# Low part of q in 128-row score tiles, adaLN rows in the weight stream's buffers

## The chip, the cores and the metric

The kernel runs on one core of a Trainium2 chip. Time is device microseconds (us) of one execution. In three runs the kernel before took 1821.42, 1823.60 and 1826.22 us; their median is 1823.6 us. A profile of one execution, with every instruction's start and length, stands beside them.

## The reference

One layer of a hybrid backbone on 512 latent tokens (64 x 8 grid, width 1024) and 256 context tokens: an adaLN-modulated norm, one input projection that feeds three mixers (neighbourhood attention, Hyena long convolution, RG-LRU), a gated merge with an output projection, then PEER expert retrieval and a last norm. The part that the change touches is the attention's scores and the modulation vectors:

```python
mod = (jax.nn.silu(c) @ w_ada[l] + b_ada[l]).reshape(B, 1, N_MOD, D)      # six vectors of 1024
s_loc = jnp.einsum('bwhd,bawkhd->bhwak', q_r, k_win) * scale + bias       # 8 heads of 64
s_ctx = jnp.einsum('bwhd,bchd->bhwc', q_r, kc) * scale
s = jnp.concatenate([s_loc, s_ctx], axis=-1)                              # softmax over both
```

All of it is float32, and a product of two operands is made from high and low parts.

## The kernel before

A float32 operand x is split into a high part rounded to the matmul's type (fp32r) and a low part x - high. A product takes three matmuls: high by high, high by low, low by high. `mm3` (lines 221 to 226) does that for the eight 128-row pieces of a weight block, 24 matmuls of 512 columns each. `load_split` (213) brings such a block: `load_raw` (206) loads 128 x 1024 floats by a DMA on SyncE's queue into one of the three buffers `wraw`; ScalarE rounds it into `wh` (line 217), VectorE subtracts into `wl` (218). `wh` and `wl` have two buffers each. A raw buffer is free when line 218 has read it.

The stages around the change, in the order of the program:

- `kproj` (676), interleaved with `rglru` (590): keys of latents and context. A PSUM tile of four 128-column projections is copied by ScalarE (682) and VectorE (683) into `k2` and `kc2`. For each head these hold 128 rows: 64 rows with the high part of k, 64 rows with its low part. For even heads the high part lies in rows 0 to 63, for odd heads in rows 64 to 127.
- The projection of q (730 to 741). `q2` has the high part of q, scaled, in both halves of the rows (738, 739), so that one matmul of 128 rows gives high q by high k plus high q by low k. `ql` has the low part of q (740), the even head of a pair in rows 0 to 63, the odd one in rows 64 to 127 of the same tile.
- `att_gen` (747): for each of four blocks of 128 queries and each of eight heads, `scores` makes a 128 x 512 tile: 256 local keys and 256 context keys. Each half takes one matmul with `q2` (763) and one with `ql` (764), which uses the 64 rows with the high part of k only:

```python
for o, kk in ((0, k2[:, h, kst[qb]:kst[qb] + 256]), (256, kc2[:, h])):
    PE.matmul(p[:, o:o + 256], q2[:, h, qs], kk, start=True, stop=False)
    PE.matmul(p[:, o:o + 256], ql[rows, h // 2, qs], kk[rows], start=False, stop=True)
```

  VectorE adds the bias (765, the bias `bt` comes by a DMA on SyncE's queue, 759) and takes the negative maximum (767), ScalarE the exponential (769), TensorE transposes it (777), ScalarE copies that (779), and TensorE multiplies with v (783). At the end of a block the output is normalised (788) and transposed (793).
- In the same stage, `gate_tanh` (800) for 16 gate blocks (weights `wgate`, 24 matmuls into `pj` each) and 8 blocks `wbrbc` (12 matmuls into `hx` each).
- In the same stage, `mod_gen` (279) for four modulation vectors: eight rows of `w_ada` (128 x 1024 floats, 512 KB each) come by DMAs on SyncE's queue into two buffers `ada` of their own (282, 283), VectorE scales and adds them into `acc` (286, 288), and 8 one-column matmuls sum over the partitions (292). That is 32 loads.

The order of instructions on each engine is not the order of the code: a scheduler takes the whole program, estimates when each instruction could start, and writes each engine's queue and the choice of buffer from that. An engine then runs its queue strictly in order. A row of an engine's queue below is one instruction, or several equal ones.

Of the kernel before, what the change touches and what calls it, by code (L numbers as in the profile page):

```python
# [9 lines left out]
F32 = mybir.dt.float32  # L10
F32R = mybir.dt.float32r
# [9 lines left out]
T = 512  # L21
D = 1024
CT = 256
KD = 8
# [131 lines left out]
def emit(ctx, tc, A, out, dbg=None):  # L156
    nc = tc.nc
    V, S, PE, GP = nc.vector, nc.scalar, nc.tensor, nc.gpsimd
# [47 lines left out]
    def load_raw(src, k=KD, pool=wp):  # L206
        r = pool.tile([128, KD, 128], F32, name="wraw", bufs=3)
        lastld[0] = nc.sync.dma_start(r[:, :k], src)
        return r
# [66 lines left out]
    def bada(m):  # L276
        return vec("bada")[:, m * 8:m * 8 + 8]

    def mod_gen(m, pool, bufs):
        acc = pool.tile([128, D], F32, name="acc", bufs=1)  # L280
        for k in range(KD):
            r = pool.tile([128, D], F32, name="ada", bufs=bufs)
            nc.sync.dma_start(r, A["wada"][m - 2, k])
            w = silu[:, k, 0:1]
            if k == 0:
                V.tensor_scalar(acc, r, w, None, ALU.mult)
            else:
                V.scalar_tensor_tensor(out=acc, in0=r, scalar=w, in1=acc, op0=ALU.mult, op1=ALU.add)
            yield
        ps = hx.tile([128, 512], F32, name="hx")  # L290
        for j in range(8):
            PE.matmul(ps[:, j:j + 1], acc[:, j * 128:j * 128 + 128], onec, start=True, stop=True)
        V.tensor_tensor(mod[:, m, :, 0], ps[:, :8], bada(m), ALU.add)
# [436 lines left out]
    mgs = ctx.enter_context(ExitStack())  # L730
    mg = open_pool(mgs, "mg", side="right")
    q2 = mg.tile([128, 8, T], F32R, name="q2")
    ql = mg.tile([128, 4, T], F32R, name="ql")
    for c in range(4):
        ps, _ = proj(c)
        for i in range(2):
            a_, b_ = slice(64 * i, 64 * i + 64), slice(64 - 64 * i, 128 - 64 * i)
            S.activation(q2[a_, 2 * c + i], ps[a_], AF.Copy, scale=0.125)
            S.activation(q2[b_, 2 * c + i], ps[a_], AF.Copy, scale=0.125)
            V.scalar_tensor_tensor(out=ql[a_, c], in0=ps[a_], scalar=0.125, in1=q2[a_, 2 * c + i],  # L740
                                   op0=ALU.mult, op1=ALU.subtract)

    yah = mg.tile([128, 4, T], F32R, name="yah")
# [3 lines left out]
    def att_gen(ap_):  # L747
        kst = [0, 64, 192, 256]
        vw = [(vt[:, 0], vt[:, 1]), (vs[:, 0], vs[:, 1]), (vs[:, 1], vs[:, 2]), (vt[:, 2], vt[:, 3])]
        for qb in range(4):  # L750
# [1 line left out]
            po = at.tile([128, 512], F32, name="po", bufs=1)  # L752
            bts = []
            def scores(h):
                rows = slice((h % 2) * 64, (h % 2) * 64 + 64)
                p = at.tile([128, 512], F32, name="at")
                if h % BH == 0:
                    bt = ap_.tile([128, BH, 256], F32, name="bt", bufs=2)
                    nc.sync.dma_start(bt, A["nab"][qb, :, h:h + BH])
                    bts.append(bt)  # L760
                qs = slice(qb * 128, qb * 128 + 128)
                for o, kk in ((0, k2[:, h, kst[qb]:kst[qb] + 256]), (256, kc2[:, h])):
                    PE.matmul(p[:, o:o + 256], q2[:, h, qs], kk, start=True, stop=False)
                    PE.matmul(p[:, o:o + 256], ql[rows, h // 2, qs], kk[rows], start=False, stop=True)  # L764
                V.tensor_add(p[:, :256], p[:, :256], bts[-1][:, h % BH])
                nm = ap_.tile([128, 1], F32, name="nm", bufs=3)
                V.tensor_reduce(nm, p, AX.X, ALU.max, negate=True)
                e = ap_.tile([128, 512], F32, name="ae", bufs=2)
                S.activation(e, p, AF.Exp, bias=nm, accum_out=sm[:, h:h + 1])
                return e  # L770
# [35 lines left out]
    with ExitStack() as st:  # L806
# [2 lines left out]

        def late_mods():  # L810
            for m in (2, 4, 3, 5):
                yield from mod_gen(m, ap_, 2)

        lm = late_mods()
        for dc in range(8):
# [490 lines left out]
```

## Time and profile before

| | |
|---|---|
| profiled execution, device time | 1826.02 us |
| its span in the profile | 1824.2 us |
| TensorE busy | 1777.0 us, 97% |
| VectorE busy | 1399.5 us, 77% |
| ScalarE busy | 788.3 us, 43% |
| mean granted TensorE clock | 0.991 of full speed |

The profile names TensorE PE (PEld are its weight loads), VectorE DVE, ScalarE ACT, GpSimd POOL and SyncE's queue SPq. Matmuls overlap in the pipeline and their printed lengths overlap too: the time that a matmul takes from the engine is the distance from its start to the next start. A granted clock of 1.00 is 2.4 GHz, 0.50 is 1.2 GHz. The names in the rows leave buffer numbers out, so `k2` is `k`, `kc2` is `kc`, `q2` is `q`. A float32 matmul that is not fp32r (783, 292) shows as two rows in the trace for one in the program.

### The profile page before, as it was taken

The page shows a single profiled execution, that of the slowest core. Times are in us where ns is not written, and L with a number is a line of the kernel's source. Part 1 is how long each engine was busy: PE and PEld are TensorE (multiplying, and loading weights), DVE is VectorE, ACT ScalarE, POOL GpSimd, SP SyncE. Part 2 cuts the span into 40 slices and gives each one's busy share as a digit, 9 for nine tenths or more (in the row PEclk, how much of TensorE's full clock was granted, in tenths as well). Part 3 has the DMA queues.
Part 4 walks back from the last instruction along what each step waited for, and adds up shares of the span by engine and source line. Part 5 has one row for each costly group of instructions (what it writes and reads, how often), then busy time and mean ns, then how long its engine had stood idle before and what let it go on. Part 6 is the DMA issues. An engine that isn't in the chain of part 4 may idle for free.

```text
span 1824.2 us, 25674 instructions
## 1 busy us (share of the span) xinstructions
PE 1777.0 (97%) x9585; PEld 1543.5 (85%) x9585; DVE 1399.5 (77%) x2550; ACT 788.3 (43%) x1140; POOL 350.9 (19%) x266
## 2 busy tenths in 40 slices
PE   7999999999999999999999999999999999999996
PEld 4688788888878889999999988888888888888885
DVE  6485564555346999999999677888887888788887
ACT  5355553333334324566677533333333333333334
POOL 0000000000000000201011123434443444344451
PEclk9999999999999999999999999999999999999999
DMA  8231522554254224757788899999999999999984
GB/s 311 68 103 47 173 75 89 171 159 130 69 159 139 93 82 138 249 185 280 273 297 290 314 373 326 325 349 334 355 341 346 325 357 340 343 340 333 325 294 155
DMA packets 157677, 431.33 MB, mean 236 GB/s; under 512 B 12784, under 2 KB 62192, under 8 KB 155504
## 3 DMA queue, kind: packets, MB, share of 16 engines
q1 hardware_dynamic: 116224, 257.44, 41.6%
q0 software_dynamic: 36864, 134.23, 20.4%
q10 hardware_dynamic: 4464, 38.01, 5.4%
q8 instruction: 75, 1.23, 0.3%
q14 instruction: 50, 0.41, 0.1%
HBM read 388.48 MB, written 41.16 MB: 236 GB/s over the span
## 4 chain that ended last, share of the span: by engine, by line
PE 87%; DVE 5%; DMA 3%; ACT 2%; issue 2%; POOL 0%; SPq 0%; DVEq 0%; ACTq 0%; POOLq 0%
PE pS L226 9%; PE pS L225 9%; PE pS L224 9%; PE ac L1221 9%; PE ac L1222 9%; PE ac L1220 9%; PE pj L224 6%; PE pj L226 6%; PE pj L225 6%; PE hx L421 2%; PE po L783 2%; DMA gr<-v_rows,idx 1%; PE hx L224 1%; PE hx L225 1%; PE at L764 1%
## 5 line engine op out<-in xcount | busy, mean ns | idle before, releaser
L217 ACT CAST wh<-wraw 128x1024 fp32r<-128x1024 f32 x340 | 350.4, 1032 | 442.2 <-PE pS L225 220.1
L218 DVE TENSOR_TENSOR wl<-wraw,wh 128x1024 fp32r<-128x1024 f32 x340 | 407.3, 1199 | 152.3 <-ACT wh L217 144.4
L1121 POOL DMA_INDIRECT gr<-u_rows,idx x128 | 172.6, 1349 | 1213.2 <-DVE db L1027 744.8
L226 PE MATMUL pS<-zh,wl 128*128 128x384 f32 x1024 | 344.9, 338 | 1.4 <-DVE wl L218 1.4
L224 PE MATMUL pS<-zh,wh 128*128 128x384 f32 x1024 | 344.2, 336 | 1.8 <-ACT sg L1104 1.8
L225 PE MATMUL pS<-zl,wh 128*128 128x384 f32 x1024 | 344.3, 336 | 0.0
L1221 PE MATMUL ac<-wl,ah 128*128 128x512 f32 x768 | 299.4, 390 | 3.1 <-DVE wl L218 3.1
L1222 PE MATMUL ac<-wh,al 128*128 128x512 f32 x768 | 299.0, 390 | 0.0
L1220 PE MATMUL ac<-wh,ah 128*128 128x512 f32 x768 | 276.1, 390 | 1.7 <-ACT wh L217 1.7
L1131 POOL DMA_INDIRECT gr<-v_rows,idx x128 | 171.7, 1341 | 218.0 <-DVE yacc L1137 192.8
L224 PEld LDWEIGHTS pS<-zh,wh 128*128 128x128 f32 x1024 | 192.4, 188 | 5.0 <-ACT sg L1104 2.3
L226 PEld LDWEIGHTS pS<-zh,wl 128*128 128x128 f32 x1024 | 192.2, 188 | 3.4 <-DVE wl L218 2.2
L225 PEld LDWEIGHTS pS<-zl,wh 128*128 128x128 f32 x1024 | 192.4, 188 | 2.7
L1221 PEld LDWEIGHTS ac<-wl,ah 128*128 128x128 f32 x768 | 144.2, 188 | 32.4 <-DVE wl L218 4.4
L1137 DVE SCALAR_TENSOR_TENSOR yacc<-gr,cf,yacc 128x1024 f32<-128x1024 f32 x126 | 160.1, 1280 | 12.6 <-DMA gr<-v_rows,idx 12.6
L1222 PEld LDWEIGHTS ac<-wh,al 128*128 128x128 f32 x768 | 144.2, 188 | 29.6
L1220 PEld LDWEIGHTS ac<-wh,ah 128*128 128x128 f32 x768 | 143.8, 188 | 29.1 <-ACT wh L217 2.0
L1123 DVE SCALAR_TENSOR_TENSOR gr<-gr,xtk 128x1024 f32<-128x1024 f32 x128 | 154.5, 1219 | 0.4 <-DMA gr<-u_rows,idx 0.3
L224 PE MATMUL pj<-xh,wh 128*128 128x512 f32 x336 | 135.2, 402 | 6.3 <-DVE k L683 3.3
L226 PE MATMUL pj<-xh,wl 128*128 128x512 f32 x336 | 135.2, 403 | 0.0
L225 PE MATMUL pj<-xl,wh 128*128 128x512 f32 x336 | 134.7, 401 | 0.0
L1096 ACT COPY stg<-pG 128x512 f32<-128x512 f32 x96 | 99.6, 1164 | 27.7 <-PE pG L1094 27.7
(388 smaller groups left out, 2626.9 us busy)
## 6 DMA issues: line engine op xcount, KB each, us to landing
wraw<-u_cols SPq DMA_DIRECT2D x128, 512.0 KB
wraw<-v_rows SPq DMA_DIRECT2D x128, 512.0 KB
ada<-wada SPq DMA_DIRECT2D x48, 512.0 KB
Gd<-stg ACTq DMA_DIRECT2D x12, 2048.0 KB
gt<-Gd SPq DMA_DIRECT2D x32, 768.0 KB
wraw<-wgate SPq DMA_DIRECT2D x24, 512.0 KB
Sd<-sg ACTq DMA_DIRECT2D x15, 768.0 KB
sgl<-Sd SPq DMA_DIRECT2D x15, 768.0 KB
```

What stands on the lines that cost most here:

```text
L217: S.copy(h[:, :k], r[:, :k])
L218: lsub[0] = V.tensor_sub(l[:, :k], r[:, :k], h[:, :k])
L224: PE.matmul(ps, wh[:, kw], xh[:, kx], start=start and j == 0, stop=False)
L225: PE.matmul(ps, wh[:, kw], xl[:, kx], start=False, stop=False)
L226: PE.matmul(ps, wl[:, kw], xh[:, kx], start=False, stop=stop and j == n - 1)
L1121: GP.indirect_dma_start(out=r, out_offset=None, in_=A["u_rows"], in_offset=bass.IndirectOffsetOnAxis(ap=idx3[:, j:j + 1], axis=0))
L1123: V.scalar_tensor_tensor(out=r, in0=r, scalar=1.0, in1=xtk, op0=ALU.mult, op1=ALU.mult, accum_out=sel3[:, j:j + 1])
L1131: GP.indirect_dma_start(out=r, out_offset=None, in_=A["v_rows"], in_offset=bass.IndirectOffsetOnAxis(ap=idx3[:, j:j + 1], axis=0))
L1137: V.scalar_tensor_tensor(out=a, in0=r, scalar=cf3[:, j:j + 1], in1=a, op0=ALU.mult, op1=ALU.add)
L1220: PE.matmul(ac[t][h], ah[:, ts], vhf[:, hs_], start=j == 0, stop=False)
L1221: PE.matmul(ac[t][h], ah[:, ts], vlf[:, hs_], start=False, stop=False)
L1222: PE.matmul(ac[t][h], al[:, ts], vhf[:, hs_], start=False, stop=j == NB - 1)
```

## The change

`ql` gets a tile of its own for each head. The half of its rows that would face the low part of k is set to zero by GpSimd once, ahead of the projection of q, and the second score matmul then uses all 128 rows of `ql` and of the keys. The rows of `w_ada` lose their two buffers; they are loaded by `load_raw` into the three buffers of the weight stream.

```diff
--- before.py
+++ after.py
@@ -276,11 +276,10 @@
     def bada(m):
         return vec("bada")[:, m * 8:m * 8 + 8]
 
-    def mod_gen(m, pool, bufs):
+    def mod_gen(m, pool):
         acc = pool.tile([128, D], F32, name="acc", bufs=1)
         for k in range(KD):
-            r = pool.tile([128, D], F32, name="ada", bufs=bufs)
-            nc.sync.dma_start(r, A["wada"][m - 2, k])
+            r = load_raw(A["wada"][m - 2, k].rearrange("p (k e) -> p k e", k=KD)).rearrange("p k e -> p (k e)")
             w = silu[:, k, 0:1]
             if k == 0:
                 V.tensor_scalar(acc, r, w, None, ALU.mult)
@@ -730,14 +729,16 @@
     mgs = ctx.enter_context(ExitStack())
     mg = open_pool(mgs, "mg", side="right")
     q2 = mg.tile([128, 8, T], F32R, name="q2")
-    ql = mg.tile([128, 4, T], F32R, name="ql")
+    ql = mg.tile([128, 8, T], F32R, name="ql")
+    for i in range(2):
+        GP.memset(ql[64 - 64 * i:128 - 64 * i, i:8:2].bitcast(F32), 0.0)
     for c in range(4):
         ps, _ = proj(c)
         for i in range(2):
             a_, b_ = slice(64 * i, 64 * i + 64), slice(64 - 64 * i, 128 - 64 * i)
             S.activation(q2[a_, 2 * c + i], ps[a_], AF.Copy, scale=0.125)
             S.activation(q2[b_, 2 * c + i], ps[a_], AF.Copy, scale=0.125)
-            V.scalar_tensor_tensor(out=ql[a_, c], in0=ps[a_], scalar=0.125, in1=q2[a_, 2 * c + i],
+            V.scalar_tensor_tensor(out=ql[a_, 2 * c + i], in0=ps[a_], scalar=0.125, in1=q2[a_, 2 * c + i],
                                    op0=ALU.mult, op1=ALU.subtract)
 
     yah = mg.tile([128, 4, T], F32R, name="yah")
@@ -752,7 +753,6 @@
             po = at.tile([128, 512], F32, name="po", bufs=1)
             bts = []
             def scores(h):
-                rows = slice((h % 2) * 64, (h % 2) * 64 + 64)
                 p = at.tile([128, 512], F32, name="at")
                 if h % BH == 0:
                     bt = ap_.tile([128, BH, 256], F32, name="bt", bufs=2)
@@ -761,7 +761,7 @@
                 qs = slice(qb * 128, qb * 128 + 128)
                 for o, kk in ((0, k2[:, h, kst[qb]:kst[qb] + 256]), (256, kc2[:, h])):
                     PE.matmul(p[:, o:o + 256], q2[:, h, qs], kk, start=True, stop=False)
-                    PE.matmul(p[:, o:o + 256], ql[rows, h // 2, qs], kk[rows], start=False, stop=True)
+                    PE.matmul(p[:, o:o + 256], ql[:, h, qs], kk, start=False, stop=True)
                 V.tensor_add(p[:, :256], p[:, :256], bts[-1][:, h % BH])
                 nm = ap_.tile([128, 1], F32, name="nm", bufs=3)
                 V.tensor_reduce(nm, p, AX.X, ALU.max, negate=True)
@@ -809,7 +809,7 @@
 
         def late_mods():
             for m in (2, 4, 3, 5):
-                yield from mod_gen(m, ap_, 2)
+                yield from mod_gen(m, ap_)
 
         lm = late_mods()
         for dc in range(8):
```

The scheduler writes other queues for the stages from `kproj` to the end of attention. After them the queues hold the same instructions in the same order as before. Three places show what moves.

VectorE in `kproj`; `l` and `lb` are tiles of `rglru`, `k` and `kc` those of the keys. Before:

```order
L639 TENSOR_TENSOR lb<-la_1644 128x256
L288 SCALAR_TENSOR_TENSOR acc<-ada,silu,acc 128x1024
L640 SCALAR_TENSOR_TENSOR l_1546<-lb,l_1546 128x256
L288 SCALAR_TENSOR_TENSOR acc<-ada,silu,acc 128x1024
L639 TENSOR_TENSOR lb<-la_1650 128x512
L683 TENSOR_TENSOR k_1233<-pj,k_1233 64x512
L640 SCALAR_TENSOR_TENSOR l_1555<-lb,l_1555 128x512
L646 TENSOR_TENSOR l_1546<-l_1546,l_1550 128x256
L288 SCALAR_TENSOR_TENSOR acc<-ada,silu,acc 128x1024
L218 TENSOR_TENSOR wl<-wraw,wh 128x1024
L639 TENSOR_TENSOR lb<-la_1656 128x256
L683 TENSOR_TENSOR kc_1234<-hx,kc_1234 64x256
```

The same place now; line 682 is what was line 683, and 638 and 639 were 639 and 640:

```order
L638 TENSOR_TENSOR lb<-la_1644 128x256
L639 SCALAR_TENSOR_TENSOR l_1546<-lb,l_1546 128x256
L638 TENSOR_TENSOR lb<-la_1650 128x512
L639 SCALAR_TENSOR_TENSOR l_1555<-lb,l_1555 128x512
L682 TENSOR_TENSOR k_1233<-pj,k_1233 64x512
L638 TENSOR_TENSOR lb<-la_1656 128x256
L645 TENSOR_TENSOR l_1546<-l_1546,l_1550 128x256
L639 SCALAR_TENSOR_TENSOR l_1564<-lb,l_1564 128x256
L647 SCALAR_TENSOR_TENSOR l_1550<-la_1644,l_1546 128x256
L218 TENSOR_TENSOR wl<-wraw,wh 128x1024
L682 TENSOR_TENSOR kc_1234<-hx,kc_1234 64x256
```

The additions of the first modulation vector, eight rows of `w_ada`, stood among the copies of the keys; now none stands there, and the first comes behind the projection of q.

SyncE's queue early in the attention stage, with the numbers of the buffers' tiles. Before:

```order
L208 DMA wraw_2118<-wgate 128x1024
L208 DMA wraw_2225<-wgate 128x1024
L208 DMA wraw_2263<-wbrbc 128x512
L759 DMA bt_2158<-nab 128x512
L208 DMA wraw_2329<-wgate 128x1024
L208 DMA wraw_2447<-wgate 128x1024
L759 DMA bt_2202<-nab 128x512
L208 DMA wraw_2485<-wbrbc 128x512
```

And now:

```order
L208 DMA wraw_2120<-wgate 128x1024
L208 DMA wraw_2153<-wada 128x1024
L208 DMA wraw_2156<-wada 128x1024
L208 DMA wraw_2227<-wgate 128x1024
L208 DMA wraw_2259<-wada 128x1024
L759 DMA bt_2160<-nab 128x512
L208 DMA wraw_2262<-wada 128x1024
L208 DMA wraw_2265<-wbrbc 128x512
L208 DMA wraw_2331<-wgate 128x1024
L208 DMA wraw_2363<-wada 128x1024
L759 DMA bt_2204<-nab 128x512
L208 DMA wraw_2366<-wada 128x1024
```

VectorE's queue at the readers of the last two rows of `w_ada` in that piece, now:

```order
L287 SCALAR_TENSOR_TENSOR acc_2152<-wraw_2363,silu_82,acc_2152 128x1024
L287 SCALAR_TENSOR_TENSOR acc_2152<-wraw_2366,silu_82,acc_2152 128x1024
L765 TENSOR_TENSOR at_2159<-at_2159,bt_2160 128x256
L218 TENSOR_TENSOR wl_2268<-wraw_2265,wh_2267 128x512
L765 TENSOR_TENSOR at_2182<-at_2182,bt_2160 128x256
L767 TENSOR_REDUCE nm_2167<-at_2159 128x1
```

Loads of `w_ada` and of weights now take turns in three buffers. `wraw_2363` and `wraw_2366` are the same buffer, so the second of the two additions (now line 287) waits for a load that can't be issued before the first has read its buffer.

TensorE at the one-column matmuls of the last modulation vector. Before:

```order
L783 MATMUL po<-vt,aeT 128x64 x2
L783 MATMUL po<-vc,aeT 128x64 x2
L777 MATMUL at<-ident,ae 128x128 x4
L763 MATMUL at<-k_1233,q_1882 128x256
L764 MATMUL at<-k_1233,ql 128x256
L763 MATMUL at<-kc_1234,q_1882 128x256
L764 MATMUL at<-kc_1234,ql 128x256
L777 MATMUL at<-ident,ae 128x128 x4
L292 MATMUL hx<-onec,acc 128x1 x8
L224 MATMUL pj<-xh,wh 128x512
L225 MATMUL pj<-xl,wh 128x512
L783 MATMUL po<-vt,aeT 128x64 x2
```

And now (line 291 was 292):

```order
L783 MATMUL po<-vt,aeT 128x64 x2
L783 MATMUL po<-vc,aeT 128x64 x2
L763 MATMUL at<-k_1233,q_1882 128x256
L764 MATMUL at<-k_1233,ql 128x256
L763 MATMUL at<-kc_1234,q_1882 128x256
L764 MATMUL at<-kc_1234,ql 128x256
L777 MATMUL at<-ident,ae 128x128 x4
L291 MATMUL hx<-onec,acc 128x1 x8
L224 MATMUL pj<-xh,wh 128x512
L225 MATMUL pj<-xl,wh 128x512
L226 MATMUL pj<-xh,wl 128x512
```

Behind them stood two matmuls of 512 columns and then more short ones; now ten of 512 columns follow. Ahead of the piece shown now stands one more pair of line 783, so two heads' worth in all.

## Rows read from the trace of the kernel before

**Rows 1.** The page, busy time of TensorE: us, share of the span, instructions.

```profile
PE 1777.0 (97%) x9585; PEld 1543.5 (85%) x9585; DVE 1399.5 (77%) x2550; ACT 788.3 (43%) x1140; POOL 350.9 (19%) x266
```

**Rows 2.** Busy time by stretch: length, each engine's busy us (instructions), clock, DMA, GB/s.

```profile
190.00:245.00 55.00, 51.66 (x255) 42.82 (x253) 40.26 (x55) 30.26 (x52) 0.00 (x0) 0.94 0.50 162
245.00:470.00 225.00, 225.00 (x1161) 183.44 (x1160) 114.62 (x163) 86.33 (x156) 0.00 (x0) 0.98 0.38 121
```

**Rows 3.** TensorE in order of time, one head's four score matmuls and the next start.

```profile
253.16 0.36 PE L763 MATMUL at<-k,q 128*128 128x256 f32 x1
253.46 0.38 PE L764 MATMUL at<-k,ql 64*128 64x256 f32 x1
...
254.39 0.50 PE L224 MATMUL pj<-xh,wh 128*128 128x512 f32 x1
```

**Rows 4.** TensorE and its weight loads in `kproj`, 256 columns with 128 rows.

```profile
217.01 0.28 PE L226 MATMUL hx<-ch,wl 128*128 128x256 f32 x1
217.13 0.28 PE L224 MATMUL hx<-ch,wh 128*128 128x256 f32 x1
...
217.13 0.19 PEld L225 LDWEIGHTS hx<-cl,wh 128*128 128x128 f32 x1
```

**Rows 5.** Who waited for whom from 190 to 475: total us, times, longest.

```profile
DVE acc L288 <- DMA ada<-wada: 18.0, 12, 2.3
...
PE pj L224 <- DVE k L683: 3.3, 1, 3.3
```

**Rows 6.** The chain of work, 205 to 225 us: start, length, what.

```profile
209.76 4.38 DMA ada<-wada
...
218.17 1.20 DVE acc L288
...
222.03 0.70 DVE k L683
```

**Rows 7.** TensorE by stretch: length, busy us, granted clock, DMA, GB/s.

```profile
222.78:228.60 5.82, 5.82 (x14) 0.50 0.44 155
357.00:362.00 5.00, 5.00 (x36) 1.00 0.38 111
447.20:457.40 10.20, 10.20 (x35) 0.50 0.08 31
```

**Rows 8.** TensorE in order of time at the last modulation vector's sum.

```profile
442.64 0.55 PE L783 MATMUL po<-vt,aeT 128*128 128x64 f32 x4
...
443.47 0.61 PE L777 MATMUL at<-ident,ae 128*128 128x128 f32 x4
443.83 0.36 PE L763 MATMUL at<-k,q 128*128 128x256 f32 x1
...
445.06 0.66 PE L777 MATMUL at<-ident,ae 128*128 128x128 f32 x4
445.56 1.98 PE L292 MATMUL hx<-onec,acc 128*128 128x1 f32 x16
447.40 0.78 PE L224 MATMUL pj<-xh,wh 128*128 128x512 f32 x1
```

**Rows 9.** VectorE in order of time; the third reads the buffer freed by the first.

```profile
316.31 0.74 DVE L286 TENSOR_SCALAR acc<-ada,silu 128x1024 f32<-128x1024 f32 x1
317.09 1.28 DVE L288 SCALAR_TENSOR_TENSOR acc<-ada,silu,acc 128x1024 f32<-128x1024 f32 x1
320.59 1.28 DVE L288 SCALAR_TENSOR_TENSOR acc<-ada,silu,acc 128x1024 f32<-128x1024 f32 x1 [2.21 <-DMA ada<-wada]
```

**Rows 10.** Groups by line and shape, 200 to 475 us: busy us, mean ns | idle before.

```profile
L217 ACT CAST wh<-wraw 128x1024 fp32r<-128x1024 f32 x24 | 25.2, 1048 | 28.1 <-PE pj L225 15.0 <-issue 7.0 <-PE hx L225 5.6
...
L765 DVE TENSOR_TENSOR at<-at,bt 128x256 f32<-128x256 f32 x32 | 13.7, 430 | 42.0 <-PE at L764 39.5 <-issue 2.4
```

**Rows 11.** Groups by line on GpSimd, whole span: busy us, mean ns | idle before.

```profile
L1202 POOL TENSOR_TENSOR x<-x,fgb 128x512 f32<-128x512 f32 x4 | 5.9, 1468 | 35.4 <-ACT xk L1201 35.4
...
masks.py:197 POOL MEMSET ident<- 128x128 f32 x1 | 0.2, 205 | 0.3 <-POOLq L1298 0.3
```

## The prediction

> **What bounds the kernel now.** I read the busy times first, then the stretches of the changed stages, then TensorE's own order of time there, and last the waits and the chain of work. TensorE is busy 97% of the span [rows 1]. In the attention stage, 245 to 470 us, it is never idle (225.00 of 225.00 us), while VectorE works 114.62 us and the DMA share is 0.38 [rows 2]. In the stage before it, 190 to 245, TensorE is idle about 3.3 us in one piece [rows 2, 5]. So what TensorE is spared in attention shortens the run, as long as the other engines and the loads keep up. The reader is to see in [rows 3] that a busy TensorE is not a fast one there: starts of score matmuls lie 0.30 to 0.31 us apart.
>
> **The score matmuls.** One head's four take from 253.16 to 254.39, that is 1.23 us, 0.31 each [rows 3]; the head at 443.83 takes the same 1.23 us until 445.06 [rows 8]. Each pair alternates a 128-row with a 64-row tile. Matmuls of the same 256 columns that all use 128 rows start 0.12 us apart although each has its own weight load of 0.19 us [rows 4]: the loads run beside the matmuls, and in the score groups they don't. With 128 rows throughout I take 0.12 for each: 0.48 us a head, 0.75 less. 4 blocks of 8 heads make 32 x 0.75 = 24.0 us (two of the heads ran at half clock; they are counted at full clock here), all on the path that sets the end, as TensorE has no idle time there. The ends: 0, if 0.31 has another cause than the row count, and 24.0; the row of equal shape is so close that I take 24.0.
>
> The Trainium skill, in "TensorE: Matmul & The Clock Gate", part 3 (What overlaps and what doesn't), says that a weight load runs beside a matmul in flight only when the two use different row groups. By that rule two 128-row tiles never overlap and the score matmuls would gain nothing. The weight loads of 0.19 us that fit into steps of 0.12 [rows 4] contradict it, so I give it only the small chance of the rival below.
>
> **The first modulation vector leaves `kproj`.** Today VectorE stops in its queue for a load of `w_ada` (209.76, 4.38 us), adds, and so the copies of the keys come late: the chain runs through an addition at 218.17 and the key copy at 222.03 [rows 6], and TensorE waits 3.3 us for that copy [rows 5]. After the wait it ran 5.82 us at a granted clock of 0.50, the 1.2 GHz level [rows 7], which costs half, 2.9 us. In the changed queue no addition stands there. From the first key copy of that tile to the second there are eight short VectorE instructions left, of which none is an addition for the modulation, and the stop of 4.38 us ahead of them is gone; that brings the second copy several us forward, ahead of the point where TensorE asks for it. I take both: 6.2 us gained. Ends: 0 if another copy is late in its place, and 6.2.
>
> **The clock at the last modulation vector.** From 442.64 to 447.40 TensorE did only short work: one head's product with v, transposes, a score group, transposes, and 16 one-column matmuls [rows 8]. Then the clock stood at 0.50 for 10.20 us [rows 7], a loss of 5.1. In the changed queue the piece has two heads' products (0.83 us each, 442.64 to 443.47), a score group of 0.48, one set of transposes (0.36) and the one-column matmuls (447.40 - 445.56 = 1.84): 4.3 us in place of 4.8. That is nearest to the piece that lost the clock, so I let it fall again. But ten matmuls of 512 columns follow, as in `kproj`, where it came back after 5.82 us; the loss is then 2.9, and 2.2 us are gained. Ends: 0 and 5.1. At the second vector's sum at 357 to 362 the clock stayed 1.00 [rows 7].
>
> **The shared buffers.** The stage has 56 loads: 32 of `w_ada`, 16 `wgate`, 8 `wbrbc`. They had five buffers and get three. From the built program I counted how many VectorE instructions lie from the one that frees a load's buffer to the one that reads the load: six or fewer for 14 of the 56 before, all of them `w_ada`; for 26 now, 8 of them weights. An instruction of this stage takes 114.62/163 = 0.70 us on average [rows 2], so six are some 4.2 us. A load took 3.5 us from the freeing instruction (316.31 + 0.74) to its reader (320.59) with little else in flight [rows 9], 4.38 in another case [rows 6], and a weight also needs 1.05 us of ScalarE [rows 10]. So VectorE will stop for loads more often than today's 12 times, 18.0 us [rows 5]. Behind such a stop wait the bias addition, the maximum and so exponential and transposes of the next head, and the second half of weights.
>
> The plainest place is the pair of additions that use one buffer in turn: VectorE stands 3.5 us between them with a head's bias addition behind. From that head's scores to its transposes TensorE has 24 matmuls of 512 columns and some short ones. A 512-column matmul is twice the columns of [rows 4], so 0.24 us each as an estimate, some 6 us of cover. VectorE also has room: today it waits 39.5 us for score matmuls in this stage [rows 10]. Part of that goes with the 24 us. Ends for the whole: 0, if cover holds everywhere as it does from 245 to 470 today, and one stall of `kproj`'s kind (3.3 us with 2.9 of half clock, 6.2) in each of the eight rounds of two gates, 49.6. I take two waits of 3.3 without a fall of the clock, 7 us: all but one of today's twelve stops passed without a TensorE wait, and twice as many are to come with less room.
>
> The eight additions that leave `kproj` (0.74 + 7 x 1.28 = 9.7 us [rows 9]) cost nothing by themselves in attention: VectorE would have 124 us of work in some 200.
>
> **The zeros.** Two memsets of 64 x 2048 floats on GpSimd, which is idle then. Its memset of 128 columns took 0.205 us [rows 11]; 16 times that is 3.3 us at most each, as part of the 0.205 is a fixed cost. By the product of 512 columns at 1.468 [rows 11] it would be 5.9. In the queues they stand ahead of the projection of q, whose first two groups, 48 matmuls of 512 columns, TensorE runs before the first score; that hides them, and I take 0. Without the cover one memset would be on the path, 3.3 to 5.9.
>
> **The sum.** 24.0 + 6.2 + 2.2 - 7 = 25.4 us. The profiled execution took 1826.0 (span 1824.2 and 1.8 around it), so 1800.6 for it. It lies 2.4 above the median of the three runs; from the median, 1823.6, the sum gives 1798. From the end of attention on, the queues are the same and only shift.
>
> **Rivals.** A change of less than 0.3%, 5.5 us, is what I count as the same.
>
> - *The ring of three buffers becomes the bound.* One stall of 6.2 us in each of eight rounds, 49.6 in all, against 32.4 gained: 1841. It decides from the sixth stall on (32.4 / 6.2 = 5.2). For it: the counts of loads with six instructions or fewer, weights among them, and that SyncE's queue is in order, so that a load for a free buffer waits behind one for a buffer in use. Against it: the DMA share of 0.38 [rows 2] and VectorE's 39.5 us of waiting on TensorE [rows 10]. With two or three such stalls it ends at 1804 to 1810, inside my range. Chance of slower: 0.05.
> - *All cover holds and the clock stays up.* 24.0 + 6.2 + 5.1 = 35.3 gained, none lost: 1788. For it: not one TensorE wait from 245 to 470 today, with twelve VectorE stops. Against: those were covered by the slow scores. Chance 0.17.
> - *The change doesn't do what it says: scores keep their step of 0.31.* Then 6.2 + 2.2 are gained, and with slow scores covering the loads as today nothing or up to 7 is lost: 1815 to 1822, take 1819. Against it: [rows 4]. By the rule of overlap above it would be this. Chance 0.06.
>
> **How the numbers follow.** My forecast, 1798, has 0.72 with 1790 to 1812 around it; together with the 0.17 at 1788 nearly all of faster is held. The range reaches down to 1787 for the full gain and up to 1812 for two stalls of 6.2 more than I took; beyond it are the ring as the bound, most of the unchanged scores, and some of the full gain. Faster by over 0.3%: 0.72 + 0.17 and half of the unchanged scores (its part below 1818), 0.92, less 0.02 of the forecast for more stalls than its range holds: 0.90. Within 0.3%: 0.05. Slower: 0.05.
>
> **What would show it.** Right: score groups of 0.48 us; line 764's form with 128 rows; no TensorE wait for the key copy at about 220 and no half clock after it; VectorE stops for loads above 18 us but TensorE waits of some 7 us from 240 to 445; attention over about 25 us earlier, later stages shifted by the same. Wrong: score steps above 0.2 us; TensorE waits in the attention stage of more than 15 us, with releasers at lines 218 and 767; a clock of 0.50 in more than two places.

## The result and the profile after

The changed kernel took 1802.07 us, the median of four runs (1793.96 to 1803.85), against 1824.91 for the kernel before beside it (1821.42 to 1827.48): a ratio of 0.9861, 95% interval 0.983 to 0.9893. Two later draws on other chips, with medians of 1799.37 and 1798.39, gave 0.9824 (0.9796 to 0.9852) and 0.9835 (0.9803 to 0.9867). The prediction, 1798 with 1787 to 1812 around it, holds all three medians. By the ratios the three draws give 25 to 32 us (by the medians themselves 23 to 32); the sum of 25.4 us is at the low end, and that it meets the first draw's ratio so closely is luck, as the part on why the prediction was right shows.

The runs of one kernel differ by more than 10 us, and in the main the mean granted clock of a run goes with it: the six runs of the changed kernel made in the first draw go from 1793.8 at 0.995 to 1803.8 at 0.992 and 1803.1 at 0.990. A stretch at 0.50 costs half its length and lowers the mean by half its share of the span, so a run's time multiplied by its mean clock is about what it would take without such stretches. I call this the time at full clock; the clock is listed to 0.001, so rounding alone can move one value by 0.9 us. Over the 63 runs of the kernel before that the experiments brought, plain times spread from 1814.7 to 1839.1, times at full clock only from 1805.0 to 1813.8, with a median of 1808.9. The 17 runs of the changed kernel have a median of 1785.0; there the product helps less, with plain times from 1793.8 to 1803.9 and times at full clock from 1781.9 to 1789.4. So a difference of 1 or 2 us between the medians of five or six runs is not told from nothing.

So two things changed: 23.9 us at full clock, and, as the plain medians of the same runs are 1830.3 and 1798.9 (31.4 apart), another 7.5 us of half clock. The prediction had 20.3 (24.0 + 3.3 - 7) and 5.1 (2.9 + 2.2).

The profiled execution took 1793.96 us with a span of 1792.2, one of the two shortest of its kernel. Its page has TensorE 29 us less busy [rows 1]:

```profile
PE 1747.6 (98%) x9585; PEld 1531.3 (85%) x9585; DVE 1398.0 (78%) x2550; ACT 787.0 (44%) x1140; POOL 355.8 (20%) x268
```

By stretch, the same two as in [rows 2]: TensorE no longer stands in the first one, and both have a clock of 1.00; in attention it is idle 3.2 us, where it was never idle before. The DMA share in the second rose from 0.38 to 0.47 and fell in the first from 0.50 to 0.21: the first modulation vector's loads moved from one to the other, and the second stretch now reaches further past the end of attention.

```profile
190.00:245.00 55.00, 54.98 (x282) 45.80 (x282) 35.33 (x53) 34.05 (x57) 3.61 (x2) 1.00 0.21 69
245.00:470.00 225.00, 221.84 (x1262) 191.40 (x1261) 131.15 (x181) 89.92 (x164) 0.00 (x0) 1.00 0.47 154
```

One head's four score matmuls, the answer to [rows 3], go from 254.53 to 255.09: 0.56 us in place of 1.23. The steps are 0.20, 0.11, 0.12 and 0.13.

```profile
254.53 0.36 PE L763 MATMUL at<-k,q 128*128 128x256 f32 x1
254.73 0.28 PE L764 MATMUL at<-k,ql 128*128 128x256 f32 x1
254.84 0.28 PE L763 MATMUL at<-kc,q 128*128 128x256 f32 x1
254.96 0.28 PE L764 MATMUL at<-kc,ql 128*128 128x256 f32 x1
255.09 0.38 PE L777 MATMUL at<-ident,ae 128*128 128x128 f32 x2
```

The weight loads show what moved. In the kernel before, the load of line 764 starts only with its own matmul, at 253.45 and 253.46 [rows 3], and so does the load behind the group, both at 254.39:

```profile
253.45 0.18 PEld L764 LDWEIGHTS at<-k,ql 64*128 64x128 f32 x1
...
254.39 0.19 PEld L224 LDWEIGHTS pj<-xh,wh 128*128 128x128 f32 x1
```

In the changed kernel the load starts some 0.12 us ahead of its matmul (254.73 and 254.84), beside the matmul before it:

```profile
254.61 0.19 PEld L764 LDWEIGHTS at<-k,ql 128*128 128x128 f32 x1
254.73 0.19 PEld L763 LDWEIGHTS at<-kc,q 128*128 128x128 f32 x1
```

Who waited for whom, 240 to 450 (total us, times, longest), against [rows 5] and the idle time in [rows 10]: VectorE stops for loads of `w_ada` more often, 15 times and 21.8 us where it was 12 and 18.0 (with the first addition of each vector, which has a line of its own, 16 and 22.5 for 13 and 18.9), and stands for scores only 12.0 us in place of 39.5. The wait for the key copy is not there. TensorE's waits in the stage come to 3.0 us, half of them for the low part of q in the middle of its projection.

```profile
DVE acc L287 <- DMA wraw<-wada: 21.8, 15, 3.7
...
DVE at L765 <- PE at L764: 12.0, 4, 4.6
...
PE pj L224 <- DVE ql L741: 1.5, 2, 0.8
DVE acc L285 <- DMA wraw<-wada: 0.7, 1, 0.7
PE pj L226 <- DVE wl L218: 0.7, 2, 0.5
PE hx L224 <- ACT wh L217: 0.4, 1, 0.4
PE pj L224 <- ACT wh L217: 0.2, 1, 0.2
...
PE at L777 <- ACT ae L769: 0.2, 1, 0.2
```

The clock by stretch, against [rows 7]: the place behind the key copy of before, and the place of the last modulation vector's sum, which is now at 425.92. Both stand at 1.00.

```profile
222.78:228.60 5.82, 5.82 (x39) 5.28 (x38) 5.66 (x9) 1.96 (x5) 0.00 (x0) 1.00 0.28 86
...
420.00:440.00 20.00, 19.41 (x116) 16.62 (x115) 7.49 (x13) 7.09 (x12) 0.00 (x0) 1.00 0.17 53
```

GpSimd's zeros, in order of time: two of 1.8 us, done 3.6 us before the first score matmul at 239.27.

```profile
231.99 3.67 POOL L734 MEMSET ql<- 64x2048 f32 x2 [230.67 <-DVE ybcl L671]
```

### The profile page after: what moved, and what is told of

The parts are those of the page before. It is cut to its first block, busy times and chain, and to the rows that moved or that the text cites. A ratio compares the mean times of both kernels' runs of the same rounds, so it can differ in the third digit from the quotient of the medians.

```text
span 1792.2 us, 25684 instructions
## 1 busy us (share of the span) xinstructions
PE 1747.6 (98%) x9585; PEld 1531.3 (85%) x9585; DVE 1398.0 (78%) x2550; ACT 787.0 (44%) x1140; POOL 355.8 (20%) x268
## 3 DMA queue, kind: packets, MB, share of 16 engines
q8 instruction: 75, 1.23, 0.3%
## 4 chain that ended last, share of the span: by engine, by line
PE 82%; DVE 6%; DMA 6%; ACT 3%; issue 3%; POOL 0%; SPq 0%; DVEq 0%; ACTq 0%; POOLq 0%
PE pS L226 9%; PE pS L225 9%; PE pS L224 9%; PE ac L1221 8%; PE ac L1220 8%; PE ac L1222 8%; PE pj L224 6%; PE pj L225 6%; PE pj L226 6%; DMA gr<-v_rows,idx 3%; PE hx L420 2%; DVE wl L218 1%; PE po L783 1%; PE pG L1093 1%; PE hx L224 1%
```

## Experiments

Each ratio is to runs of the kernel before on the same chip, with its 95% interval; one chip served the first four, another the next four, a third the two after them, a fourth the last two. Differences at full clock are from the kernel before on the same chip, if nothing else is said.

### 128 rows alone

```diff
-PE.matmul(p[:, o:o + 256], ql[rows, h // 2, qs], kk[rows], start=False, stop=True)
+PE.matmul(p[:, o:o + 256], q2[:, h, qs], kk, start=False, stop=True)
```

> The kernel before with one edit: the second matmul of each score pair takes the 128 rows of q2 again in place of the 64 rows of ql. It leaves out the low part of q and counts the high part twice; every tile of the scores has 128 rows, and the buffers and VectorE's order are those of before. Theory (the 64-row tile between 128-row tiles is what makes the score steps 0.31 us): groups of 0.48 to 0.56 us as in the changed kernel, 21 to 24 us less than before in the scores, the wait for the key copy at about 220 still there with its half clock; a ratio of 0.987 to 0.989, some 1803 us. Rival 1 (the zeros and the new buffers give the gain, the tile shape does not): groups stay at 1.23 us and the time at 1825. Rival 2 (the slow scores covered the loads of w_ada): groups of 0.55, but 5 to 15 us come back as TensorE waits between 245 and 440, 1808 to 1818.

Measured: 1806.72 us, ratio 0.9862 (0.9822 to 0.9902); at full clock 1785.2 against 1808.9, 23.7 less. All score groups together took 17.8 us against 40.5 before. The key copy is waited for as before, and TensorE's other waits in attention are 1.0 us:

```profile
PE pj L224 <- DVE k L683: 3.2, 1, 3.2
PE hx L224 <- ACT yah L796: 0.7, 1, 0.7
PE pj L224 <- DVE ql L740: 0.3, 1, 0.3
```

TensorE's order is that of the kernel before except between 245 and 270 us. The rows of the tiles give the whole score term; no zeros and no shared buffers are needed for it. Rival 1 falls, and rival 2 too.

### The shared buffers alone

```diff
-r = pool.tile([128, D], F32, name="ada", bufs=bufs)
-nc.sync.dma_start(r, A["wada"][m - 2, k])
+r = load_raw(A["wada"][m - 2, k].rearrange("p (k e) -> p k e", k=KD)).rearrange("p k e -> p (k e)")
```

> The kernel before with the other half of the change alone: the rows of w_ada pass through the three raw buffers, the scores keep their 64-row tiles. Theory (the eight additions that leave the key projection free TensorE of a wait of 3.3 us and of the half clock after it, and the slow scores cover the stops for loads): no wait at about 220, clock 1.00 there, score groups of 1.23 us, TensorE waits in attention below 2 us; 6 us less, ratio 0.9965, 1819. With the clock also staying up at the last one-column sums 11 less, 1814. Rival 1 (the ring costs what it gives): waits of 4 us or more with releasers at the weight halves or transposes, ratio 1.000 and above. Rival 2 (nothing depends on the buffers): the wait at 220 stays, ratio 1.000.

Measured: 1822.06 us, ratio 0.9963 (0.9941 to 0.9986), 6.7 us less by the ratio (3 to 11 by its interval); at full clock 2.4 less. The wait at 220 is gone, as is the half clock behind it, and TensorE waits 0.7 us in all from 190 to 470. But at the last modulation vector's sum the clock fell, although TensorE's order in the whole stage is that of the changed kernel, with ten matmuls of 512 columns behind the sum:

```profile
190.00:245.00 55.00, 55.00 (x280) 45.55 (x279) 35.17 (x52) 34.05 (x56) 0.00 (x0) 1.00 0.27 80
...
446.50:453.50 7.00, 7.00 (x26) 6.03 (x25) 0.28 (x2) 0.45 (x2) 0.00 (x0) 0.51 0.07 26
```

The theory of the key copy holds: no wait and no half clock there. The 6.7 us lie near the 6.2 that the prediction gave it, but only 2.4 of them are time at full clock, where the wait was to give 3.3; the rest is half clock, at this place and at others.

### The same four matmuls with fewer turns

```diff
+pair = [(q2[:, h, qs], kk), (ql[rows, h // 2, qs], kk[rows])]
+if o:
+    pair.reverse()
-PE.matmul(p[:, o:o + 256], q2[:, h, qs], kk, start=True, stop=False)
-PE.matmul(p[:, o:o + 256], ql[rows, h // 2, qs], kk[rows], start=False, stop=True)
+PE.matmul(p[:, o:o + 256], *pair[0], start=True, stop=False)
+PE.matmul(p[:, o:o + 256], *pair[1], start=False, stop=True)
```

> The kernel before, with the order of the second pair of each score group turned round: high, low, low, high in place of high, low, high, low. The same four matmuls, the 64-row ones now next to each other, so two changes of tile shape in a group fall away. Theory A (each change between a 128-row and a 64-row tile costs some 0.17 us, a quarter of 1.23 - 0.55): a group of 0.85 to 0.9 us, 32 x 0.35 = 11 us less, 1814. Theory B (a 64-row matmul is slow by itself, wherever it stands): a group of 1.23 us as before, 1825; the low one after the low one still 0.3 us behind it.

Measured: 1815.35 us, ratio 0.9935 (0.9905 to 0.9964); at full clock 12.2 less. A head's group takes 0.96 us, more than the 0.85 to 0.9 of theory A. TensorE in order of time:

```profile
311.16 0.36 PE L766 MATMUL at<-k,q 128*128 128x256 f32 x1
311.46 0.38 PE L767 MATMUL at<-k,ql 64*128 64x256 f32 x1
311.68 0.28 PE L766 MATMUL at<-kc,ql 64*128 64x256 f32 x1
311.89 0.39 PE L767 MATMUL at<-kc,q 128*128 128x256 f32 x1
312.12 0.60 PE L780 MATMUL at<-ident,ae 128*128 128x128 f32 x4
```

Half of the turns gone, half of the gain there: theory A. The groups alone give 32 x 0.27 = 8.6 us. The group now ends on 128 rows, and a 512-column matmul behind it takes 0.23 us to the next start where it took 0.34 in the kernel before (254.39 to 254.73); counted with such steps, the timeline gives 11 us. The place of the cost was not quite what I wrote: the steps are 0.30, 0.22, 0.21, 0.23, so the low matmul behind the low one still takes 0.22, not 0.12. A turn costs in the step that it ends and in the one behind it, about 0.1 us each.

### Four score matmuls of 64 rows

```diff
-PE.matmul(p[:, o:o + 256], q2[:, h, qs], kk, start=True, stop=False)
+PE.matmul(p[:, o:o + 256], q2[rows, h, qs], kk[rows], start=True, stop=False)
```

> The kernel before with all four score matmuls on 64 rows: the high part of q and k enters with 64 of its 128 rows, so the low part of k is left out. Every step inside a group is then between tiles of the same shape. Theory A (the change of shape costs): steps of 0.12 to 0.14 us, a group of 0.5 to 0.6 us and some 0.2 at its ends, 15 to 22 us less than before, 1803 to 1810. Theory B (64-row matmuls are slow by themselves, 0.34 us more than 128-row ones): steps of 0.4 us and more, a group of 1.7 to 1.9, 15 to 22 us more than before, 1840 to 1847. If 0.31 is the time of any pair whose second is of 64 rows, 1825.

Measured: 1811.29 us, ratio 0.9909 (0.9872 to 0.9947); at full clock 15.7 less. With all four of 64 rows the inner steps are 0.11 to 0.12 us, so a 64-row matmul is not slow. What is left sits at the ends: the transposes ahead take 0.57 us to the first score matmul where they took 0.39 in the kernel before (313.44 to 313.83), and the last step is 0.21.

```profile
313.75 0.63 PE L777 MATMUL at<-ident,ae 128*128 128x128 f32 x4
314.32 0.38 PE L763 MATMUL at<-k,q 64*128 64x256 f32 x1
314.54 0.28 PE L764 MATMUL at<-k,ql 64*128 64x256 f32 x1
314.66 0.27 PE L763 MATMUL at<-kc,q 64*128 64x256 f32 x1
314.77 0.28 PE L764 MATMUL at<-kc,ql 64*128 64x256 f32 x1
314.98 0.66 PE L777 MATMUL at<-ident,ae 128*128 128x128 f32 x4
```

Against the group of all 128 rows this is 0.18 ahead of the group, 0.10 in it (0.66 for 0.56) and 0.05 to 0.11 in the step behind it, some 10 us over all groups as an estimate; 23.7 - 15.7 is 8.0. About 1 us comes back in a way that none of the theories had. At three places the scores of two heads stand side by side. The two use different halves of the rows, and here they run at the same time: eight matmuls in 0.67 us (412.45 to 413.12), where eight of 128 rows took 1.03 in the changed kernel and in the first experiment. In the rows below, each x2 is two matmuls, one of each head, that start 0.01 us apart.

```profile
412.45 0.40 PE L763 MATMUL at<-k,q 64*128 64x256 f32 x2
412.67 0.29 PE L764 MATMUL at<-k,ql 64*128 64x256 f32 x2
412.79 0.29 PE L763 MATMUL at<-kc,q 64*128 64x256 f32 x2
412.91 0.29 PE L764 MATMUL at<-kc,ql 64*128 64x256 f32 x2
413.12 0.50 PE L224 MATMUL hx<-ybch,wh 128*128 128x512 f32 x1
```

Theory B falls: the change between 64 and 128 rows is what costs. The Trainium skill says in "TensorEngine Tiling (Array Packing)", Key Properties, that changing the tiling mode drains the engine, and gives no price. The trace agrees with a cost at the change; a group with four turns takes 0.67 us more than one with none, 0.17 a turn; by the third and fourth experiment, with two turns each, it is 0.20 and 0.14. With the steps behind the groups counted in, all three lie between 0.17 and 0.20.

### The changed kernel again

No edit; the kernel beside the next three on their chip.

> The changed kernel once more, beside the next three on one chip. Theory (the scores give 22 to 24, the key projection 6, and the shared buffers take some of it back): ratio to the kernel before 0.985 to 0.988. Theory of the clock (runs of one program differ by the stretches at the 1.2 GHz level): the run's time times its mean granted clock agrees within some 4 us over all its runs and is 22 to 23 us below that of the kernel before, while the plain times spread over 10 us. Rival (the first six runs were a lucky draw): ratio above 0.990.

Measured: 1799.37 us, ratio 0.9824 (0.9796 to 0.9852), a little under what I wrote; at full clock 1786.7 against 1810.0, 23.3 less. The spread was not as the theory of the clock had it: in these six runs the plain times lie within 3.8 us and the products within 6.8 (1781.9 to 1788.7), so here the product tells nothing more than the time. The two halves by themselves gave 23.7 + 2.4 = 26.1 on the first chip, so putting them together loses 2.8 by these medians, which is within their noise.

### Own buffers, additions late

```diff
-PE.matmul(p[:, o:o + 256], ql[rows, h // 2, qs], kk[rows], start=False, stop=True)
+PE.matmul(p[:, o:o + 256], q2[:, h, qs], kk, start=False, stop=True)
...
-V.scalar_tensor_tensor(out=ql[a_, c], in0=ps[a_], scalar=0.125, in1=q2[a_, 2 * c + i],
+lq = V.scalar_tensor_tensor(out=ql[a_, c], in0=ps[a_], scalar=0.125, in1=q2[a_, 2 * c + i],
...
-step(lm, 2)
+with tc.issue_after(lq.ins):
+    step(lm, 2)
```

> The 128-row scores with q2 in both matmuls (the low part of q is left out), two buffers of their own for the rows of w_ada as before, and the first addition held until the last ql is written, so that none stands in the key projection. Buffers: five, as before; order: as after. Theory (sharing three buffers costs the changed kernel what lies between its 25 us and the sum of the two halves, 25.2 + 6.7 = 31.9): 31 to 33 us less than before, ratio 0.982 to 0.983, TensorE waits in attention under 1 us. Rival 1 (sharing costs nothing; the half of the buffers gives less once the scores are fast): as the changed kernel, 0.985 to 0.987. Rival 2 (late additions press on the end of attention): TensorE waits at the last additions, 0.987 and above.

Measured: 1797.64 us, ratio 0.981 (0.9781 to 0.9839); at full clock 1785.6, 1.1 less than the changed kernel beside it. TensorE waits 1.5 us in the stage. The ratio falls just under the theory's span, but its distance from the changed kernel, 1.1 at full clock and 1.7 by the medians, is nearer to rival 1: sharing three buffers costs 1 to 3 us, and the intervals don't tell this from nothing. This version also holds the first addition, which by the experiments on that below may be worth some of it.

### A fourth buffer

```diff
-BH = 2
+BH = 1
...
+if k % 2:
     r = load_raw(A["wada"][m - 2, k].rearrange("p (k e) -> p k e", k=KD)).rearrange("p k e -> p (k e)")
+else:
+    r = pool.tile([128, D], F32, name="ada", bufs=1)
+    nc.sync.dma_start(r, A["wada"][m - 2, k])
...
-ya = ap_.tile([128, 8, 64], F32, name="ya", bufs=1)
+ya = ap_.tile([128, 512], F32, name="aeT", bufs=2).rearrange("p (h e) -> p h e", e=64)
...
-step(lm, 2)
+with tc.issue_after(lq.ins):
+    step(lm, 2)
```

> The changed kernel with a fourth buffer for loads: even rows of w_ada have one of their own, odd ones pass through the three raw buffers; the first addition is held until the last ql is written. Room for it comes from bias tiles of one head in place of two and from keeping the attention output in a buffer of the transposed exponentials. Theory (the waits left in attention, 3 us by the profile after, come from three buffers for 56 loads): they fall to 1 us or less and the time is 2 to 6 us under the changed kernel, ratio 0.983 to 0.985. Rival (those waits come from the order of VectorE's queue, not from the number of buffers): 3 us of waits stay, ratio as the changed kernel. A third: twice as many bias loads and the shared output buffer cost more than the fourth buffer gives, ratio 0.988.

Measured: 1800.22 us, ratio 0.983 (0.9796 to 0.9864); at full clock 1788.3, 1.6 more than the changed kernel. VectorE's largest group of stops for loads is down to 14.5 us, 8 times, and TensorE's waits are 2.1 us, other ones than before. The fourth buffer gives nothing that can be measured; what its room cost was not tried by itself.

### Two buffers

```diff
-r = pool.tile([128, KD, 128], F32, name="wraw", bufs=3)
+r = pool.tile([128, KD, 128], F32, name="wraw", bufs=2)
```

> The changed kernel with two raw buffers in place of three, in all stages. Theory (the ring is near to being the bound; behind a stop of 3.5 us for a load TensorE has some 6 us of cover): VectorE's stops for loads go from 21.8 us to 50 or more and TensorE waits 15 to 40 us in attention; with the weights of the other stages also short of a buffer the time is 20 to 60 us above the changed kernel, ratio 0.998 to 1.02. Rival (there is much room): TensorE waits under 6 us in attention, ratio below 0.992, most of the loss outside attention.

Measured: 1826.47 us, ratio 0.998 (0.996 to 1.0); at full clock 20.8 more than the changed kernel. TensorE is idle 5.5 us in attention:

```profile
245.00:470.00 225.00, 219.54 (x1245) 187.85 (x1244) 130.83 (x180) 90.85 (x164) 0.00 (x0) 1.00 0.49 154
```

From the first matmul of the last long stage (664.6 here, 661.9 in the changed kernel's run beside it) to the end it took 1154.4 us against 1135.2: 19.2 of the 21.9 us between the two spans are lost there, where weights pass through the same buffers. The total is what my theory had, 20 us and more and a ratio of 0.998, but not for its reason: VectorE's stops for `w_ada` came to 24.0 us and not 50, and TensorE's waits in attention to 5.3, none over 0.8, and not 15 to 40. On those, and on the place of the loss, the rival holds, though not on its ratio: in attention even a ring of two costs little.

### Both halves without the zeros

```diff
-r = pool.tile([128, D], F32, name="ada", bufs=bufs)
-nc.sync.dma_start(r, A["wada"][m - 2, k])
+r = load_raw(A["wada"][m - 2, k].rearrange("p (k e) -> p k e", k=KD)).rearrange("p k e -> p (k e)")
...
-PE.matmul(p[:, o:o + 256], ql[rows, h // 2, qs], kk[rows], start=False, stop=True)
+PE.matmul(p[:, o:o + 256], q2[:, h, qs], kk, start=False, stop=True)
```

> Both halves of the change without the zeros: the rows of w_ada pass through the three raw buffers, and the second score matmul takes q2 again (the low part of q is left out), so ql keeps its four tiles of 64-row halves and GpSimd writes no zeros. TensorE's order is that of the changed kernel. Theory (the zeros are hidden ahead of the projection of q): as the changed kernel, ratio 0.981 to 0.985, time times clock 1785 to 1788. Rival (the zeros hold up the first scores): 3 us or more faster, time times clock 1783 or less. For the clock at the last one-column sums: as the changed kernel it has ten 512-column matmuls behind them and fast scores ahead; if the fast scores keep the clock up, no stretch at 1.2 GHz between 425 and 440; if it is chance, one of 3 us or more there.

Measured: 1796.36 us, ratio 0.9829 (0.9802 to 0.9855); at full clock 1785.6, as the changed kernel's 17 runs (1785.0). TensorE's order is that of the changed kernel but for 240 to 265 us. The zeros cost nothing that can be measured. The clock behind the last sums, 425 to 440, stayed up:

```profile
425.00:440.00 15.00, 14.41 (x81) 1.00 0.16 52
```

### The first addition held

```diff
-V.scalar_tensor_tensor(out=ql[a_, 2 * c + i], in0=ps[a_], scalar=0.125, in1=q2[a_, 2 * c + i],
+lq = V.scalar_tensor_tensor(out=ql[a_, 2 * c + i], in0=ps[a_], scalar=0.125, in1=q2[a_, 2 * c + i],
...
-step(lm, 2)
+with tc.issue_after(lq.ins):
+    step(lm, 2)
```

> The changed kernel with the first addition for w_ada held until the last ql is written. The profile after shows TensorE waiting 1.5 us for ql at about 248 and 256. Theory (additions that stop for loads ahead of the ql writes cause these waits): they fall under 0.5 us and nothing comes in their place, 1 us less than the changed kernel by time times clock, which the plain times cannot tell apart: ratio 0.981 to 0.984. Rival (the held additions are late at the end of attention): new waits of 2 us or more between 400 and 450, ratio 0.985.

Measured: 1797.18 us, ratio 0.9824 (0.9802 to 0.9847); at full clock 1783.6. The waits for the low part of q are gone and 1.4 us of others are left:

```profile
PE hx L224 <- ACT yah L796: 0.7, 1, 0.7
PE pj L226 <- DVE wl L218: 0.4, 1, 0.4
PE at L793 <- DVE ya L788: 0.3, 1, 0.3
```

That is 1.4 below the changed kernel's 1785.0, but on another chip, so both ran once more on one, with the same edit.

> The changed kernel, to stand beside the next one on one chip. Both theories: time times clock 1785 to 1788, ratio to the kernel before 0.981 to 0.986; TensorE waits for ql of 1 to 2 us at about 248 and 256.

> The version with the first addition held, a second time, beside the changed kernel on one chip. Theory (the held addition spares TensorE the waits for ql and some of those for weights): time times clock 2 to 4 us below that of the changed kernel, 1782 to 1785. Rival (the first comparison was of two chips): time times clock equal within 1 us.

Measured: the changed kernel 1798.39 us, ratio 0.9835 (0.9803 to 0.9867), the held one 1795.04, 0.9824 (0.9795 to 0.9854). At full clock 1784.6 and 1784.3: the rival. In the two profiles TensorE waits 3.3 us from 190 to 470, 1.8 of it for the low part of q, and 2.0, none of it for that. If holding the addition gives anything, it is about 1 us, and no run here shows it.

## Why the prediction was right, point by point

- **Scores, 24.0.** Right in cause and nearly in size. The steps inside a group are 0.12, as taken from [rows 4], but the first step of a group, behind other work, stays at 0.20, so a group takes 0.56 and not 0.48: 32 x 0.67 = 21.4. Summed over all groups it is 40.5 - 18.4 = 22.1, some of it from the two heads at half clock in the kernel before. At full clock the edit alone gives 23.7. The rest is in the step behind a group, which the prediction left out: a 512-column matmul there takes 0.34 us before and 0.24 after, transposes 0.50 (445.06 to 445.56 in [rows 8]) and 0.44 (425.48 to 425.92). Summed over the timeline these steps take 11.1 us in the kernel before and 8.7 in the first experiment, 2.4 less, so two terms that it missed nearly cancel, and 24.0 is closer than its working was. By the rule of overlap that the prediction weighed, from the Trainium skill's "TensorE: Matmul & The Clock Gate", part 3, all-128-row groups would have stayed at 0.31; the trace decides against it, as [rows 4] did.
- **The key copy, 6.2.** Right in cause: no other copy is late in its place. The shared buffers alone gave 6.7 by the ratio, of which 2.4 at full clock for the 3.3 of wait. One reading was off: the 4.38 us of [rows 6] are the load; VectorE worked for the first part of them and stopped for 2.3, the longest stop of [rows 5]. Every profile with additions among the key copies (the kernel before and the first, third and fourth experiment) shows a stretch at 0.50 between 220 and 234; none of the ten without them does.
- **The clock at the last modulation vector, 2.2.** Here the step "I let it fall again" failed. It fell in the four profiles with 64-row scores (before and the second to fourth experiment), for 3.4 us in the first experiment, and in none of the nine others, all with 128-row scores. The first experiment has the kernel before's order there and fast scores, and lost 1.7 us where that lost 5.1. The second experiment and the changed kernel have the same order of TensorE's instructions there and differ on TensorE in the 64-row tiles alone: with them 0.51 over 7 us, without them 1.00. So the gain in the profiled run is the whole 5.1 (10.20 at half clock in [rows 7]). Fast scores alone don't hold the clock: behind an earlier one-column sum it fell for 3 to 7 us in three versions that have them (first experiment from 393, own buffers from 394, fourth buffer from 347), so what decides it is not shown. Each profile is one run; over all runs, half clock cost 1830.3 - 1808.9 = 21.4 us before and 1798.9 - 1785.0 = 13.9 after, 7.5 less, where 5.1 were forecast for both places.
- **The shared buffers, -7.** The step "two waits of 3.3" was the mis-sized term. VectorE's stops did become more, 15 and 21.8 us for 12 and 18.0, but their longest is 3.7 us and TensorE's whole waiting is 3.0, of which 1.5 for the low part of q, a place I had not named. By the sum of the halves the sharing costs 2.8 us, by the experiment with own buffers 1.1, and neither is clear of noise. The 6 us of cover that I estimated behind one head's scores fits this, and nearly holds even with a ring of two (5.3 us of waits).
- **The zeros, 0.** Right; 1.8 us each, under the bound of 3.3, and hidden.

The two misses, 3 us at the clock and 4 to 6 at the buffers, go the same way, and the first term is high by under 1 us at full clock. That is why the later draws, at 30 to 32 us, lie beyond the 25.4 of the sum. In the first draw the four runs of the kernel before, with a median of 1824.9, lay under the 1830.3 of the 63, and those of the changed kernel, 1802.1, over the 1798.9 of its 17; that brought the ratio back to 25.4. Of the rivals, "all cover holds and the clock stays up" had the mechanism of the attention stage better than my forecast did: its 35.3 us make 1790.7 of the profiled 1826.0, my sum 1800.6, and the changed kernel's profile has 1793.96. The gains of the later draws lie between the two. Other stretches of half clock come and go from run to run: this profile has them only at 14 to 22 us and at the end of the span, where every profile has one, while the profile of the changed kernel run again also has two between 88 and 118.

## What to carry to other kernels

Where small matmuls take longer than their columns, look first whether neighbours differ in the number of rows: padding with zeros to one shape, or only turning the order so that like stands by like, buys back the change of shape or, as in the third experiment, half of it. Price a stall on an engine that is not the bound by the longest single stop against the cover behind it, not by the number of stops. And compare runs by time and granted clock together: over the 63 runs of the kernel before, the plain times spread over 24 us, their products with the clock over 9; over the 17 of the changed kernel it was 10 and 7.5, so look first whether it helps.

## What the runs showed of the hardware that was not expected

- A 256-column matmul of 64 rows behind another of 64 rows starts 0.12 us later, like one of 128 rows; where 128 and 64 rows alternate every step is 0.30 or 0.31, and in a group of 128, 64, 64 and 128 rows they are 0.30, 0.22, 0.21 and 0.23: the step between the two of 64 pays too.
- Two 64-row score matmuls on different halves of the rows ran at the same time: eight in 0.67 us, where eight of 128 rows took 1.03. The kernel before has its low parts in such halves, but always with a 128-row matmul between them.
- The same order of TensorE's work kept a clock of 1.00 at one place when its score matmuls ran in 0.12 us steps, and fell to 0.51 over 7 us there when they took 0.31. That is three profiles of the changed kernel against one, and at other places the clock fell with 0.12 us steps too.
